# Queries as seven block products for eight, value weights in buffers of their own, two query jobs inside the attention, squares added on GpSimd

## The chip, the cores and the metric

The kernel runs on one core of one Trainium2 chip. The metric is the device time of one execution in microseconds; for the kernel before it is 1610.38 (median of three runs, 1609.49 to 1611.93). Engines go by the profile's names: PE (TensorE, with PEld for its weight loads), DVE (VectorE), ACT (ScalarE), POOL (GpSimd), SP (SyncE, here only an issuer of loads).

## The reference

One decoder layer on x of 1024 tokens x 1024 channels, in float32. Two branches (a state-space scan and an mLSTM) are merged by gates; the change begins where the merged activations are projected:

```python
x = x + merged @ w_out[l]                       # output projection
h = _rmsnorm(x, x_norm_g[l])
x = x + _cross_attn(h, _rmsnorm(mem, mem_norm_g[l]), x_wq[l], x_wkv[l], x_wo[l])
...
def _cross_attn(h, mem_n, wq, wkv, wo):         # 4 heads of 256 channels, 256 memory tokens
    q = (h @ wq).reshape(Bsz, L, X_HEADS, X_HEAD_DIM)
    k, v = jnp.split(mem_n @ wkv, 2, axis=-1)
    s = jnp.einsum('blhd,bmhd->bhlm', q, k) * (X_HEAD_DIM ** -0.5)
    o = jnp.einsum('blhm,bmhd->blhd', softmax(s), v)
    return o @ wo
```

Then a gated convolution FFN (up and down projection) and a last norm.

## The kernel before

Activations lie transposed: channels on 128 partitions, 1024 tokens along a row; a tile of 128 channels is one "n" or "k" (eight of them), the halves H0 and H1 are tokens 0 to 511 and 512 to 1023. A float32 product is made of three matmuls on rounded parts: ACT casts an operand to its high part, DVE subtracts to get the low part (`split`), and PE adds high x high, high x low and low x high (`gemm_part`). So each weight that is loaded (`load_w`: a load on SP's queue into a raw buffer WR, a cast to WH on ACT, a subtraction to WL on DVE) occupies all three engines; WR, WH and WL have two buffers each.

The stages around the change, in program order:

1. *Output projection* (`out_job`, 14 jobs). The product is made block-wise, as 2 x 2 blocks with seven products for eight (a Strassen scheme). A block splits the channels in even and odd tiles and the tokens in halves. The seven products (p = 1 to 7) take sums of the blocks of the input (`out_sums`, on DVE) and of the weight (made in DRAM by DMAs with accumulation that POOL issues long before: table Ow), and their results are added with signs when they leave PSUM. `out_x` finishes a tile half of x: DVE adds the residual, ACT and DVE make its scaled high and low part for the queries (`scaled_split`), ACT squares it, DVE adds the square to a running sum for the norm (L1064), and a DMA stores it to X1d. Products 5 and 4 are the last four jobs.
2. *Queries, keys, values.* The order is written out in the list `QKV`: q is a plain query tile (`q_tile`, 8 k-steps x 3 x 2 halves = 48 matmuls of 128x512 in an M bank of PSUM), k a key tile (24 matmuls of 128x256), v one k-step of the values (12 matmuls of 128x512 into four A banks, L1177). a0 and a1 are the first score tiles of the attention. All their weights go through WR, WH and WL.
3. *Attention.* Eight units (two token halves x four heads): scores and softmax (`att_probs`, PE, then reductions on DVE and exponentials on ACT), transposes on PE, and the product with the values (`att_values`). From the fifth unit on, the projection of the first half (`o_tile`) lies in between.
4. *FFN up and down*, again with block products for part of the columns; their weight sums (tables Uq and Dd) are made in DRAM by the same kind of DMAs.

Those DRAM sums stand in one list (`slow_sums`: 16 for the gates, 16 for Ow, 32 for Uq, 40 for Dd), and `next_sum` issues one of them at a time on POOL's queue, tied to the last matmul before it; `sums_on` switches this on in chosen stages. A build-time scheduler then sets each engine's final order within what the dependences allow, so the order on an engine is not that of the source: before, query and key tiles are interleaved on PE at places, and the last query tile stands among the first score tiles.

Buffers are pools of fixed size: S (24 of 128x1024), R (4), Z (6), VV (4), Y (18 of 128x512), and in PSUM two M and four A tiles.

## Time and profile before

| | |
|---|---|
| median of 3 runs | 1610.38 us |
| profiled execution, its own time | 1610.51 us |
| its span, first to last instruction | 1608.7 us |
| PE busy | 1581.0 us, 98%, 7935 matmuls |
| DVE busy | 1128.8 us, 70% |
| ACT busy | 752.4 us, 47% |
| POOL busy | 173.3 us, 11% |
| output projection ends | about 665 us |
| query, key and value products | about 662 to 810 us |
| attention | about 795 to 905 us |

Times in the trace count from the start of the span. "Busy" is the time in which an engine has an instruction running. A row of a timeline has start, length, engine, line, operation, output<-inputs, shapes, count, and in square brackets the idle time before it with what ended it. A row of a group has the count, the busy time, the mean of one in ns, and the idle time before it with its releasers. The chain of waits follows the work that ended last back to the start. In the names of tiles, WR<-in_w_vv_dram is a load into WR; M and A are PSUM.

### The profile page before, as it was taken

To read this page: it belongs to the slowest core of one execution; us is meant where nothing else is said; L and a number is where in the kernel's file an instruction comes from. 1 tells how busy PE (TensorE), PEld (TensorE's weight loads), DVE (VectorE), ACT (ScalarE), POOL (GpSimd) and SP (SyncE) were. 2 spreads that over 40 slices of the span, in tenths; PEclk is the share of its full clock that TensorE was granted. 3 is DMA by queue.
4 is the path that set the end of the run, shared out by engine and by line. 5 is a ranking of instruction groups with operands and counts; after the bars stand their busy time and mean duration, and the time that the engine had idled before them with its cause. 6 is when DMAs were issued, how large, how long until landed. Compare 5 with 4: busy or idle time off the path is not lost.

```text
span 1608.7 us, 21077 instructions
## 1 busy us (share of the span) xinstructions
PE 1581.0 (98%) x7935; PEld 1329.2 (83%) x7935; DVE 1128.8 (70%) x1802; ACT 752.4 (47%) x1231; POOL 173.3 (11%) x258
## 2 busy tenths in 40 slices
PE   9999999999999999999999999999999999999997
PEld 7898888888888788878888887888878888888887
DVE  7868867666565799734266469799888777867635
ACT  6446555633463437523254246444444444653413
POOL 1001111000101101000100000000111011121014
PEclk9999999999999999999999999999999999999998
DMA  6255655634987568555444458753787376876312
GB/s 196 99 147 130 154 129 127 153 99 131 294 303 183 144 156 247 182 159 157 92 140 169 128 180 254 204 150 98 208 199 192 110 183 189 295 272 210 118 40 105
DMA packets 101222, 270.55 MB, mean 168 GB/s; under 512 B 11136, under 2 KB 25152, under 8 KB 101120
## 3 DMA queue, kind: packets, MB, share of 16 engines
q1 hardware_dynamic: 66592, 160.75, 29.5%
q0 software_dynamic: 26992, 94.12, 25.8%
q10 hardware_dynamic: 7536, 14.33, 2.3%
q8 instruction: 62, 1.02, 0.3%
q14 instruction: 40, 0.33, 0.1%
HBM read 234.04 MB, written 106.43 MB: 212 GB/s over the span
## 4 chain that ended last, share of the span: by engine, by line
PE 85%; DMA 5%; DVE 4%; ACT 3%; issue 2%; POOL 0%; POOLq 0%; SPq 0%; ACTq 0%; DVEq 0%
PE M L220 29%; PE A L1408 12%; PE M L1408 10%; PE M L1555 6%; PE A L1084 5%; PE A L1555 5%; PE A L891 4%; PE A L220 3%; PE M L307 1%; DMA S<-in_w_up_dram 1%; DMA WR<-in_w_vv_dram 1%; PE A L1275 1%; PE A L1219 1%; DMA WR<-in_w_uq_dram 1%; DVE WL L185 1%
## 5 line engine op out<-in xcount | busy, mean ns | idle before, releaser
L220 PE MATMUL M<-S,WH 128*128 128x512 f32 (+1 forms) x1352 | 363.2, 381 | 3.1 <-DVE dc L802 1.4
L220 PEld LDWEIGHTS M<-S,WH 128*128 128x128 f32 x1352 | 246.4, 188 | 51.4 <-DVE Y L185 2.3
L184 ACT CAST WH<-WR 128x1024 fp32r<-128x1024 f32 (+2 forms) x115 | 109.5, 953 | 242.1 <-PE M L220 121.9
L220 PE MATMUL M<-S,WL 128*128 128x512 f32 (+1 forms) x676 | 213.3, 379 | 1.2 <-DVE WL L185 1.2
L185 DVE TENSOR_TENSOR WL<-WR,WH 128x1024 fp32r<-128x1024 f32 (+2 forms) x115 | 126.6, 1102 | 96.4 <-ACT WH L184 95.2
L220 PEld LDWEIGHTS M<-S,WL 128*128 128x128 f32 x676 | 126.9, 188 | 24.8 <-DVE WL L185 1.7
L1408 PE MATMUL M<-S,Y 128*128 128x512 f32 x468 | 111.9, 389 | 0.0
L1408 PEld LDWEIGHTS M<-S,Y 128*128 128x128 f32 x468 | 87.9, 188 | 18.2
L1431 DVE SCALAR_TENSOR_TENSOR S<-Z,cols,S 128x1023 f32<-128x1023 f32 (+1 forms) x72 | 90.8, 1280 | 7.1 <-ACT S L1429 7.0
L1408 PE MATMUL M<-S,W 128*128 128x512 f32 x324 | 78.4, 389 | 0.0
L184 ACT CAST W<-Y 128x512 fp32r<-128x512 f32 x51 | 31.6, 620 | 92.5 <-PE A L1408 74.0
L1408 PE MATMUL A<-S,W 128*128 128x512 f32 x288 | 70.9, 389 | 0.7 <-ACT W L184 0.7
L1408 PEld LDWEIGHTS M<-S,W 128*128 128x128 f32 x324 | 60.7, 188 | 12.9 <-DVE Z L1425 0.3
L1084 PE MATMUL A<-S,WH 128*128 128x512 f32 x224 | 67.7, 390 | 0.0
L891 PE MATMUL A<-S,WH 128*128 128x512 f32 x224 | 67.1, 390 | 0.0
L1408 PEld LDWEIGHTS A<-S,W 128*128 128x128 f32 x288 | 54.0, 188 | 12.2 <-ACT W L184 1.1
L211 POOL DMA_DIRECT2D Dd<-in_w_dq_dram x30 | 19.2, 642 | 388.3 <-PE M L220 134.9
L1408 PE MATMUL A<-S,Y 128*128 128x512 f32 x240 | 59.9, 389 | 0.0
L185 DVE TENSOR_TENSOR S<-S,S 128x512 fp32r<-128x512 f32 x79 | 52.2, 691 | 8.6 <-ACT S L184 8.4
L1555 PE MATMUL M<-S,W 128*128 128x512 f32 x240 | 57.8, 389 | 0.0
L1408 PE MATMUL A<-R,W 128*128 128x512 f32 x228 | 56.6, 391 | 0.3 <-ACT Z L1415 0.3
L184 ACT CAST S<-S 128x512 fp32r<-128x512 f32 x79 | 46.2, 618 | 21.2 <-PE M L1555 6.2
(509 smaller groups left out, 3401.4 us busy)
## 6 DMA issues: line engine op xcount, KB each, us to landing
Uq<-in_w_uq_dram POOLq DMA_DIRECT2D x24, 512.0 KB, 6.4
Dd<-in_w_dq_dram POOLq DMA_DIRECT2D x24, 512.0 KB, 5.1
Td<-Gq POOLq DMA_DIRECT2D x24, 512.0 KB, 8.6
WR<-in_w_in_dram SPq DMA_DIRECT2D x21, 512.0 KB, 4.1
Gq<-S SPq DMA_DIRECT2D x18, 512.0 KB, 4.6
WR<-in_w_o_dram SPq DMA_DIRECT2D x16, 512.0 KB, 3.3
...
```

The costliest lines, as they stand in the source:

```text
L184: A.copy(out=hi, in_=src)
L185: (lo_eng or V).tensor_tensor(out=lo, in0=src, in1=hi.bitcast(F32), op=ALU.subtract)
L211: d = nc.gpsimd.dma_start(out=out, in_=in_, **kw)
L220: last_mm[0] = PE.matmul(ps[:, s:e], lhsT, rhs[:, s:e], start=first and is_first, stop=last and is_last)
L307: PE.matmul(pus[j][h.start // 512], w_[:, 0, j * P : (j + 1) * P], x_[:, h], start=k == 0 and f, stop=k == KD - 1 and l)
L891: last_mm[0] = PE.matmul(ps[q], w[:, 0, c], x, start=f, stop=l, skip_group_check=True)
L1084: last_mm[0] = PE.matmul(ps[q], w[:, 0, c], x, start=f, stop=l, skip_group_check=True)
L1219: PE.matmul(ps[:, i * NM : (i + 1) * NM], lhsT[:, tok], rhs, start=f, stop=l)
L1275: last_mm[0] = PE.matmul(po, lhsT[:, ns], rhs, start=f, stop=l)
L1408: up_mm[0] = PE.matmul(ps, lhsT[:, c], rhs, start=f, stop=l, skip_group_check=True)
L1431: V.scalar_tensor_tensor(out=acc[:, d_:], in0=raw[:, : T - d_], scalar=col("fcw", 3 * ct + 2 - d_), in1=acc[:, d_:], op0=ALU.mult, op1=ALU ...
L1555: paced[0] = PE.matmul(dps[p][n], lhsT[:, c], rhs, start=f, stop=l, skip_group_check=True)
```

## The change

- *Queries as block products.* The query weights come in blocks (`w_qq`), 14 jobs (`q_job`: product p, column group g; p in the order 1, 3, 2, 6, 7, 4, 5) of 24 matmuls replace eight tiles of 48. Products 1, 3 and 2 need plain blocks of x (`out_x` makes the parts of those blocks only, 12 scaled splits for 16); 6, 7, 4 and 5 need sums, made by `q_sums` (8 ACT scalings and 16 DVE additions in all, in place in the x tiles that were stored) and split by `q_turn` (16 splits). The results are put together on leaving PSUM and split for the attention (`q_out`). The weight sums are a fourth table, Qw, with 16 more DRAM sums ahead of those for Uq.
- *Value weights.* `load_w` takes a raw buffer: value weights are loaded into Z tiles and split into VV tiles, no longer through WR, WH and WL; `qkv_weights` asks for each kind of weight one step ahead.
- *Two jobs in the attention.* Jobs 12 and 13 (product 5, for the second half of the tokens) are called in units 0 and 2.
- *Squares.* The 14 additions of squares in `out_x` are on POOL.
- *Sums.* `next_sum` is called once per query job, once in each of the first units, and behind six tiles of the second half's projection.
- The FFN, its weights and the stages before the output projection are as before.

The core of the diff:

```diff
-    "q0 k0 v0 k1 v1 q1 k2 v2 k3 v3 q2 k4 v4 k5 v5 q3 k6 v6 k7 v7 q4 q5 q6 a0 a1 q7 "
+Q_LATE = {0: 12, 2: 13}
+V_FROM = 1
+    "j0 s0 j1 k0 s1 v0 s2 j2 s3 k1 v1 t60 j3 t61 k2 t62 v2 t63 j4 x0 k3 t70 v3 t71 j5 k4 t72 v4 t73 j6 k5 t40 v5 t41 j7 t42 k6 v6 t43 j8 k7 v7 t50 j9 t51 t52 t53 j10 j11 a0 a1 "
...
-    def load_w(src, shape, alloc=None):
+    def load_w(src, shape, alloc=None, raw=None):
...
-        raw = wp.tile([P, T], F32, tag="WR", name=nm("WR"))[:, :fw]
+        raw = wp.tile([P, T], F32, tag="WR", name=nm("WR"))[:, :fw] if raw is None else raw
...
     def out_x(n, h, u, ps):
-        x = Y()
+        i, odd = n // 2, n % 2
+        x = qraw[i, odd, h] = Y() if odd or h else qe0[i // 2][:, H[i % 2]]
         V.tensor_tensor(out=x, in0=u, in1=ps, op=ALU.add)
-        hi, lo = x1g[n]
-        scaled_split(x, col("x_g", n) if n % 2 == h else nxg[:, n : n + 1], hi[:, H[h]], lo[:, H[h]])
+        if odd or not h:
+            t = (S if odd else VV)(F32R)
+            qp[1 + odd + odd * h, i] = scaled_split(x, col("x_g", n) if odd == h else nxg[:, n : n + 1], t[:, H[0]], t[:, H[1]])
...
-            V.tensor_tensor(out=sq1[h], in0=sq1[h], in1=t, op=ALU.add)
+            G.tensor_tensor(out=sq1[h], in0=sq1[h], in1=t, op=ALU.add)
...
+    def q_sums(i):
+        e0, e1, o0, o1 = (qraw[i, x, h] for x in range(2) for h in range(2))
+        n = 2 * i + 1
+        for e, g_ in ((e0, col("x_g", n - 1)), (e1, nxg[:, n - 1 : n])):
+            A.activation(out=e, in_=e, func=AF.Copy, scale=g_)
+        V.scalar_tensor_tensor(out=o1, in0=o1, scalar=nxg[:, n : n + 1], in1=e1, op0=ALU.mult, op1=ALU.add)
+        V.tensor_tensor(out=e1, in0=e0, in1=e1, op=ALU.add)
+        V.tensor_tensor(out=e0, in0=e0, in1=o1, op=ALU.add)
+        V.scalar_tensor_tensor(out=o0, in0=o0, scalar=col("x_g", n), in1=e0, op0=ALU.mult, op1=ALU.add)
...
+    def q_job(k):
+        p, g = qjobs[k]
+        wh, wl = qws.pop((p, g))
+        ps_ = psM()
+        ps = [ps_[:, H[0]], ps_[:, H[1]]]
+        for q in range(2):
+            for i in range(4):
+                c = slice(512 * q + P * i, 512 * q + P * i + P)
+                xh, xl = qp[p, i]
+                for w, x, f, l in ((wh, xh, i == 0, False), (wh, xl, False, False), (wl, xh, False, i == 3)):
+                    last_mm[0] = PE.matmul(ps[q], w[:, 0, c], x, start=f, stop=l)
+        if k in Q_SUM:
+            next_sum()
+        add, sub = ALU.add, ALU.subtract
+        if p in (1, 3):
+            t = (qu if p == 1 else qr)[g] = S()
+            A.copy(out=t, in_=ps_)
+        elif p in (6, 7):
+            V.tensor_tensor(out=qu[g], in0=qu[g], in1=ps_, op=sub if p == 6 else add)
+            if p == 6:
+                V.tensor_tensor(out=qr[g], in0=qu[g], in1=qr[g], op=sub)
+        else:
+            for q in range(2):
+                n, u = 4 * g + 2 * q, qu[g][:, H[q]]
+                if p == 2:
+                    t = Y()
+                    V.tensor_tensor(out=t, in0=u, in1=ps[q], op=add)
+                    q_out(n, 0, t)
...
+                else:
+                    r = qr[g][:, H[q]]
+                    V.scalar_tensor_tensor(out=r, in0=ps[q], scalar=-1.0, in1=r, op0=ALU.mult, op1=sub)
+                    V.tensor_tensor(out=u, in0=u, in1=ps[q], op=add)
+                    q_out(n, 1, r)
+                    q_out(n + 1, 1, u)
...
+                kvw[c, n] = load_w(a["w_vv"][n].unsqueeze(1), (1, D), VV, raw=Z())
...
-        wh, wl = load_w(a["w_vv"][k].unsqueeze(1), (1, D))
+        wh, wl = kvw.pop(("v", k))
...
         probs(u + 1, 0)
+        if u in Q_LATE:
+            q_job(Q_LATE[u])
+        elif u < 4:
+            next_sum()
         t_ = att_turn(pes.pop(u))
```

What the scheduler makes of it, at three places (names with numbers are single tiles).

PE, the end of a key tile (M_941) and the value step behind it, before; WH, WL are the shared homes:

```order
L220 MATMUL M_941_6068<-S_834_5501,WH_939_6064 128x256
L220 MATMUL M_941_6068<-S_835_5502,WH_939_6064 128x256
L220 MATMUL M_941_6068<-S_834_5501,WL_940_6065 128x256
L1177 MATMUL A_919_5941<-WH_944_6099,S_831_5482 128x512
L1177 MATMUL A_920_5942<-WH_944_6099,S_831_5482 128x512
L1177 MATMUL A_921_5943<-WH_944_6099,S_831_5482 128x512
L1177 MATMUL A_922_5944<-WH_944_6099,S_831_5482 128x512
L1177 MATMUL A_919_5941<-WL_945_6100,S_831_5482 128x512
L1177 MATMUL A_920_5942<-WL_945_6100,S_831_5482 128x512
L1177 MATMUL A_919_5941<-WH_944_6099,S_832_5483 128x512
```

PE now, around a query job (M_956, L1200); L1267 is the value step, on weights in VV:

```order
L1267 MATMUL A_911_5926<-VV_938_6060,S_831_5523 128x512
L1267 MATMUL A_912_5927<-VV_938_6060,S_831_5523 128x512
L1267 MATMUL A_911_5926<-VV_937_6059,S_832_5524 128x512
L1267 MATMUL A_912_5927<-VV_937_6059,S_832_5524 128x512
L1200 MATMUL M_956_6183<-S_866_5731,WH_945_6123 128x512 x2
L1267 MATMUL A_909_5924<-VV_950_6158,S_831_5523 128x512
L1267 MATMUL A_910_5925<-VV_950_6158,S_831_5523 128x512
L1200 MATMUL M_956_6183<-S_866_5731,WL_946_6124 128x512
L1200 MATMUL M_956_6183<-S_870_5744,WH_945_6123 128x512 x2
L1200 MATMUL M_956_6183<-S_870_5744,WL_946_6124 128x512
```

The value matmuls no longer read WH and WL, and two of the next step stand between the query job's first matmuls and those that need its low weights WL_946.

DVE at the end of the output projection, from the first eviction of product 5 (A_881), before; L1064 adds squares, WL_892 is a weight of the last output jobs:

```order
L1056 TENSOR_TENSOR Y_883_5746<-S_782_5224,A_881_5720 128x512
L1056 TENSOR_TENSOR Y_884_5752<-S_818_5427,A_881_5720 128x512
L275 SCALAR_TENSOR_TENSOR S_870_5702<-Y_883_5746,cols_75,S_869_5701 128x512
L1056 TENSOR_TENSOR Y_886_5760<-S_782_5224,A_882_5721 128x512
L275 SCALAR_TENSOR_TENSOR VV_773_5186<-Y_884_5752,nxg_4846,VV_772_5185 128x512
L1064 TENSOR_TENSOR Z_720_4845<-Z_720_4845,Y_885_5756 128x512
L1056 TENSOR_TENSOR Y_888_5768<-S_818_5427,A_882_5721 128x512
L185 TENSOR_TENSOR WL_892_5779<-WR_890_5776,WH_891_5778 128x1024
L1056 TENSOR_TENSOR Y_896_5813<-S_789_5270,A_894_5787 128x512
L275 SCALAR_TENSOR_TENSOR S_872_5704<-Y_886_5760,cols_75,S_871_5703 128x512
L1064 TENSOR_TENSOR Z_720_4845<-Z_720_4845,Y_887_5764 128x512
L275 SCALAR_TENSOR_TENSOR VV_775_5188<-Y_888_5768,nxg_4846,VV_774_5187 128x512
```

DVE now, from the same eviction (A_863); L1171 to L1173 are sums of query inputs:

```order
L1060 TENSOR_TENSOR Y_865_5729<-S_776_5219,A_863_5703 128x512
L1060 TENSOR_TENSOR Y_867_5736<-S_808_5418,A_863_5703 128x512
L252 TENSOR_SCALAR ms_836_5560<-M_837_5561 128x2
L278 SCALAR_TENSOR_TENSOR S_866_5731<-Y_865_5729,cols_75,S_866_5731 128x512
L1060 TENSOR_TENSOR Y_869_5742<-S_776_5219,A_864_5704 128x512
L1060 TENSOR_TENSOR Y_872_5751<-S_808_5418,A_864_5704 128x512
L188 TENSOR_TENSOR WL_876_5760<-WR_874_5757,WH_875_5759 128x1024
L278 SCALAR_TENSOR_TENSOR S_870_5744<-Y_869_5742,cols_75,S_870_5744 128x512
L1060 TENSOR_TENSOR Y_880_5794<-S_783_5265,A_878_5768 128x512
L1171 SCALAR_TENSOR_TENSOR Y_865_5729<-Y_865_5729,nxg_4847,Y_867_5736 128x512
L1060 TENSOR_TENSOR Y_883_5803<-S_818_5467,A_878_5768 128x512
L1172 TENSOR_TENSOR Y_867_5736<-R_721_4849,Y_867_5736 128x512
```

POOL now, at the same time:

```order
L253 TENSOR_TENSOR rm_4851<-ms_836_5560,mhalf_99 128x2
L1069 TENSOR_TENSOR Z_720_4846<-Z_720_4846,Y_868_5738 128x512
L1069 TENSOR_TENSOR Z_720_4846<-Z_720_4846,Y_871_5747 128x512
L1069 TENSOR_TENSOR Z_720_4846<-Z_720_4846,Y_873_5753 128x512
L1069 TENSOR_TENSOR Z_720_4846<-Z_720_4846,Y_882_5799 128x512
L1069 TENSOR_TENSOR Z_720_4846<-Z_720_4846,Y_884_5805 128x512
L1069 TENSOR_TENSOR Z_720_4846<-Z_720_4846,Y_887_5814 128x512
L1069 TENSOR_TENSOR Z_720_4846<-Z_720_4846,Y_889_5820 128x512
```

The square additions have left DVE for POOL, where seven follow each other behind the norm of the memory; in their place DVE has the input sums.

PE at the first score tiles (L1219, the last query tile M_1051 behind them), before:

```order
L1219 MATMUL A_1045_6864<-Z_722_4852,S_927_6002 128x256
L1219 MATMUL A_1045_6864<-R_721_4851,S_927_6002 128x256
L1219 MATMUL A_1045_6864<-R_721_4851,S_950_6172 128x256
L1219 MATMUL A_1045_6864<-Z_722_4852,S_950_6172 128x256
L1219 MATMUL A_1045_6864<-R_721_4851,S_950_6172 128x256
L220 MATMUL M_1051_6891<-VV_772_5185,WH_1049_6887 128x512 x2
L220 MATMUL M_1051_6891<-VV_773_5186,WH_1049_6887 128x512 x2
L220 MATMUL M_1051_6891<-VV_772_5185,WL_1050_6888 128x512 x2
```

PE now: score tiles (L1305), then job 12 (M_1103):

```order
L1305 MATMUL A_1100_6969<-R_933_6045,S_976_6312 128x256
L1305 MATMUL A_1100_6969<-R_933_6045,S_1065_6853 128x256
L1305 MATMUL A_1100_6969<-Z_934_6046,S_1065_6853 128x256
L1305 MATMUL A_1100_6969<-R_933_6045,S_1065_6853 128x256
L1200 MATMUL M_1103_6990<-S_1050_6769,WH_1095_6959 128x512 x2
L1200 MATMUL M_1103_6990<-S_1050_6769,WL_1096_6960 128x512
L1200 MATMUL M_1103_6990<-S_1055_6805,WH_1095_6959 128x512 x2
L1200 MATMUL M_1103_6990<-S_1055_6805,WL_1096_6960 128x512
```

Where one query tile stood there are now the two jobs of product 5, M_1103 and, behind it, M_1134.

More of the change, by code (lines that the diff above doesn't have):

```diff
@@ L220, in gemm_part, with ntile @@
                 last_mm[0] = PE.matmul(ps[:, s:e], lhsT, rhs[:, s:e], start=first and is_first, stop=last and is_last)
-    def ntile(src, xs, nk=KD, width=T, w=None, order=None):
+    def ntile(src, xs, nk=KD, width=T, w=None):
         wh, wl = w or load_w(src, (nk, P))
         ps = psM()
-        for i, k in enumerate(order or range(nk)):
-            gemm_part(ps, (wh[:, k, :], wl[:, k, :]), xs[k][0], xs[k][1], width, i == 0, i == nk - 1)
-            if i % 4 == 3:
-                next_sum(i // 4)
+        for k in range(nk):
+            gemm_part(ps, (wh[:, k, :], wl[:, k, :]), xs[k][0], xs[k][1], width, k == 0, k == nk - 1)
+            if k % 4 == 3 and width == T:
+                next_sum(k // 4)
         return ps
@@ new lines, in hybrid_layer, with qkv_weights @@
+    Kt, kv_k = [None, None], {}
+    kvw, asked = {}, set()
+    def qkv_weights(i, kinds, ahead):
+        for step in QKV[i:]:
+            c, n = step[0], int(step[1:])
+            if c not in kinds:
+                continue
+            if not ahead:
+                break
+            ahead -= 1
+            if step in asked:
+                continue
+            asked.add(step)
+            if c == "j":
+                q_weights(n)
+            elif c == "k":
+                kvw[c, n] = load_w(a["w_k"][n], (KD, P))
+            else:
+                kvw[c, n] = load_w(a["w_vv"][n].unsqueeze(1), (1, D), VV, raw=Z())
@@ L1163, in k_tile @@
     def k_tile(n):
-        ps = ntile(a["w_k"][n], mhv, width=NM)
+        ps = ntile(None, mhv, width=NM, w=kvw.pop(("k", n)))
+        Kt[n // 4] = Kt[n // 4] or (R(F32R), Z(F32R))
+        kv_k[n] = [t[:, (n % 4) * NM : (n % 4) * NM + NM] for t in Kt[n // 4]]
         kf = Y()[:, :NM]
@@ L1187, in hybrid_layer @@
     sums_on[0] = 0
-    x1g += [(VV(F32R)[:, :T], VV(F32R)[:, :T]) if n in (0, 2) else None for n in range(KD)]
     for k, (p, g) in enumerate(ojobs):
@@ L1193, in hybrid_layer @@
             out_turn(OUT_TURNS[k])
-        if k in (2, 10):
-            for n in range(k == 10, KD, 2):
-                x1g[n] = x1g[n] or (S(F32R), S(F32R))
         if k == MEM_AT:
@@ L1232, in hybrid_layer @@
     pv = [psA() for _ in range(4)]
-    for step in QKV:
-        n = int(step[1])
+    sums_on[0] = 1
+    qkv_weights(0, "j", 1)
+    for i_, step in enumerate(QKV):
+        n = int(step[1:])
+        if step[0] in "jkv":
+            qkv_weights(i_ + 1, "jk", 1)
+            if i_ > V_FROM:
+                qkv_weights(i_ + 1, "v", 1)
         if step[0] == "k":
             k_tile(n)
-        elif step[0] == "q":
-            q_tile(n)
+        elif step[0] == "x":
+            x1_norm()
+        elif step[0] == "s":
+            q_sums(n)
+        elif step[0] == "t":
+            q_turn(n // 10, n % 10)
+        elif step[0] == "j":
+            k = n
+            q_job(k)
         elif step[0] == "a":
-            if not n:
-                x1_norm()
             pes.setdefault(0, []).append(att_probs(2 * n, 0))
@@ L1581, in weights @@
             down_w(k - len(jobs))
+    for k in Q_LATE.values():
+        q_weights(k)
+    sums_on[0] = 0
     units = [(half, h) for half in range(2) for h in range(4)]
```

55 lines of the change are left out of this document (34 added, 21 removed).

## Prediction

> **What bounds the kernel now.** I read the page first, then the busy time by stage, then the chain of waits, then single stretches in order of time. The page gives the bound at once:
>
> ```profile
> PE 1581.0 (98%) x7935; PEld 1329.2 (83%) x7935; DVE 1128.8 (70%) x1802; ACT 752.4 (47%) x1231; POOL 173.3 (11%) x258
> ```
>
> PE is busy for 98% of the span, so the time is the number of matmuls times their pace, plus the few places where PE waits. The busy time by stage (span of the stretch, then PE, PEld, DVE, ACT and POOL busy with their counts, granted clock, DMA share, GB/s) shows where the change works: output projection to 662, query, key and value products to 810, attention to 905, then the joint of the last two, and ten-microsecond pieces of the end of the output projection.
>
> ```profile
> 582.00:662.00 80.00, 79.75 (x356) 65.81 (x355) 71.11 (x109) 55.19 (x96) 7.94 (x11) 1.00 0.68 211
> 662.00:810.00 148.00, 143.87 (x731) 120.33 (x730) 58.45 (x84) 45.30 (x68) 11.95 (x17) 1.00 0.52 139
> 810.00:905.00 95.00, 93.64 (x518) 80.36 (x517) 62.60 (x113) 48.14 (x108) 2.61 (x4) 1.00 0.45 150
> 800.00:840.00 40.00, 38.64 (x236) 33.56 (x235) 25.86 (x54) 21.84 (x58) 3.31 (x5) 1.00 0.39 97
> 650.00:660.00 10.00, 10.00 (x46) 8.28 (x45) 10.00 (x16) 9.14 (x15) 0.00 (x0) 1.00 0.58 192
> 660.00:670.00 10.00, 10.00 (x46) 8.29 (x45) 10.00 (x15) 6.85 (x11) 0.00 (x0) 1.00 0.58 203
> ```
>
> PE hardly rests anywhere, at a granted clock of 1.00. DVE has room in the query stage (58.45 of 148 us) and none at all from 650 to 670 us, where the output projection ends. What a matmul costs stands in the chain of waits, where PE runs without a wait (start, length, line, count):
>
> ```profile
> 647.87 14.54 PE A L1084 x64
> ...
> 761.36 32.65 PE M L220 x144
> ```
>
> The second row is three whole query tiles: 32.65/144 = 0.227 us for a 128x512 matmul; the first, in the output projection, gives the same 14.54/64 = 0.227.
>
> **Part 1: fewer matmuls.** A query tile has 8 k-steps x 3 products x 2 halves = 48 matmuls, eight tiles 384. The seven block products have 2 column groups x 2 x 4 x 3 = 24 matmuls in each of 14 jobs, 336. So 48 go: 48 x 0.227 = **-10.9 us**. The new program's PE has 48 instructions fewer (7498 for 7546 in order), and all those removed were at the full 512 width, on the engine that sets the end; nothing hides them.
>
> **Part 2: value weights.** In order of time, PE's key tile and the value step behind it:
>
> ```profile
> 679.18 1.19 PE L1177 MATMUL A<-WH,S 128*128 128x512 f32 x4 [0.25 <-ACT WH L184]
> ...
> 683.24 0.40 PE L220 MATMUL M<-S,WH 128*128 128x256 f32 x2
> ...
> 685.64 0.28 PE L220 MATMUL M<-S,WL 128*128 128x256 f32 x1
> 688.06 1.20 PE L1177 MATMUL A<-WH,S 128*128 128x512 f32 x4 [2.14 <-ACT WH L184]
> ```
>
> ```profile
> PE A L1177 <- ACT WH L184: 3.2, 3, 2.1
> ```
>
> ```profile
> DMA to landing us min/median/max: 3.5/4.6/6.5
> ```
>
> PE stood 2.14 us for the cast of a value weight, whose load had taken 3.5 to 6.5 us to land (last row, of the value-weight loads), since loads of queries, keys and values share two raw and two split homes. The rows from 679.18 to the three query tiles at 761.36 (82.2 us) hold eight value steps (96 matmuls at 0.227 = 21.8), three query tiles (144, 32.7) and seven key tiles (168 at 0.12, from 20 matmuls between 683.24 and 685.64: 20.2): 74.7 us. So 7.6 us are lost there, the visible waits and the slow first matmuls behind them (1.20 us for four). With a home of its own a value weight is loaded and split some steps ahead, and the new order of PE even slips single value matmuls into a query job while its low part is being made. But 14 query jobs instead of 8 tiles make more joints of two short pieces, each with a fresh weight. Bounds: 0 to 7.6 us back; I take **-4.5**, most of the value waits and not the joints.
>
> **Part 3: what DVE and ACT get.** Durations:
>
> ```profile
> L185 DVE TENSOR_TENSOR WL<-WR,WH 128x1024 fp32r<-128x1024 f32 x91 | 111.1, 1222 | 93.9 <-ACT WH L184 92.7 <-issue 0.6 <-PE A L307 0.5
> L184 ACT CAST WH<-WR 128x1024 fp32r<-128x1024 f32 x91 | 95.5, 1051 | 225.2 <-PE M L220 112.6 <-issue 28.6 <-PE A L220 15.8
> ...
> L185 DVE TENSOR_TENSOR S<-Y,S 128x512 fp32r<-128x512 f32 x40 | 26.2, 689 | 3.6 <-ACT S L184 3.5
> ...
> L1760 POOL TENSOR_TENSOR Z<-Z,Y 128x512 f32<-128x512 f32 x7 | 9.1, 1296 | 61.7 <-ACT Y L1756 61.2
> ```
>
> DVE: 6 more weights split (x 1.22 = 7.3), 16 sums of inputs and 16 splits of them (32 x 0.69 = 22.1), 6 evictions of 1024 (7.3) and 16 of 512 (11.0), 4 scaled splits fewer (-2.8): +44.9 us, and 14 squares fewer (-9.7). ACT: 6 casts, 4 copies of 1024, 20 more of 512, about +23. From 662 to 905 DVE is busy 121 of 243 us; 35 more leave it at two thirds. Step by step it also fits: behind a job of products 2 or 4 DVE has two evictions and one weight to do (2 x 0.6 + 1.14 at the pace below, 2.3 us) while PE does a key tile (24 x 0.12 = 2.9 us). So I put this part at 0, covered by key tiles; without that cover a job would lose up to 2.3 us.
>
> **Part 4: squares on GpSimd.** Fourteen additions of 1.296 us move to POOL, which has room. What they may cost shows at the end of the program, where POOL adds squares already (first row POOL, the others DVE; start, length):
>
> ```profile
> 1570.73 4.05 POOL L1760 TENSOR_TENSOR Z<-Z,Y 128x512 f32<-128x512 f32 x3 [3.46 <-ACT Y L1756]
> ```
>
> ```profile
> 1571.70 0.41 DVE L1751 TENSOR_TENSOR VV<-VV,A 128x256 f32<-128x256 f32 x1
> 1572.89 0.42 DVE L1751 TENSOR_TENSOR VV<-VV,M 128x256 f32<-128x256 f32 x1 [0.78 <-PE M L220]
> 1573.80 1.27 DVE L1760 TENSOR_TENSOR Z<-Z,Y 128x256 f32<-128x256 f32 x1 [0.48 <-ACT Z L1753]
> 1574.99 0.41 DVE L1751 TENSOR_TENSOR VV<-VV,M 128x256 f32<-128x256 f32 x1
> 1575.32 0.41 DVE L1760 TENSOR_TENSOR Z<-Z,Y 128x256 f32<-128x256 f32 x1
> ```
>
> While POOL added (until 1574.78), the DVE additions that read one operand from PSUM (VV,A and VV,M) took their usual 0.41; the one with both operands in SBUF took 1.27 and ended just after POOL did; the same addition later took 0.41. So DVE loses about 0.9 us to a POOL addition whenever its next operation reads SBUF twice. Eleven of the fourteen fall in the last four output jobs, where DVE is full, and the order puts the new sums and the weight splits among them, which all read SBUF twice. DVE's pace there:
>
> ```profile
> 646.10 1.29 DVE L1056 TENSOR_TENSOR Y<-S,A 128x512 f32<-128x512 f32 x2 [1.13 <-PE A L1084]
> ...
> 667.14 0.69 DVE L1056 TENSOR_TENSOR Y<-S,A 128x512 f32<-128x512 f32 x1
> 667.73 1.23 DVE L185 TENSOR_TENSOR WL<-WR,WH 128x1024 fp32r<-128x1024 f32 x1
> 668.87 0.76 DVE L275 SCALAR_TENSOR_TENSOR S<-Y,nxg,S 128x512 fp32r<-128x512 f32 x1
> 669.53 0.69 DVE L1064 TENSOR_TENSOR Z<-Z,Y 128x512 f32<-128x512 f32 x1
> ```
>
> From start to start: 0.60 for an addition of 512, 1.14 for a weight, 0.66 for a scaled one. From the eviction of product 5 (646.10) to the low part of the first query job's weights the new order has 9 evictions and 5 sums at 0.60, 7 scaled operations at 0.66, 3 weights at 1.14: 16.4 us, with about 1 us of waiting for PE, ready at 663.5. PE needs it when the output projection ends, about 665.5: 2 us of slack. Some eight of the eleven POOL additions lie before that point, three more before the next job's weights. Below: 0, if they meet evictions only or POOL lags. Above: 11 x 1.296 - 2 = 12.3. I take 11 x 0.9 = 9.9 less the 2 of slack and about 2.5 that the key and value steps behind the first two jobs absorb: **+5.5 us**. In the measured stretches up to 646 PE lost nothing to a full DVE, so the 9.7 us that DVE is spared buy nothing.
>
> [...]
>
> **Part 5: two jobs in the attention.** The last jobs (product 5) are only needed by the second half of the tokens and fill PE where softmax waits. Before, the eighth query tile did that: 40 us at the joint hold 1.36 us of idle PE. But the tile cost DVE one weight and two splits (2.6 us), the two jobs cost two weights, eight evictions, eight splits (13.5 us), in order ahead of reductions and transposes that PE waits for. In 810 to 905 DVE has 32 us free, so at most a few single waits: 0 to 4, I take **+1.5**.
>
> **Part 6: loads.** Six more weight loads of 512 KB and 16 more DRAM sums. The sums push the last 16 of the table Uq behind them, into the query jobs and attention:
>
> ```profile
> L1377 SPq DMA_DIRECT2D Y<-Uq x32: 319/320/656, 973.6 to 1062.7; - x32
> L211 POOL DMA_DIRECT2D Uq<-in_w_uq_dram x24: 520/542/844, 356.9 to 582.4; - x24
> ```
>
> They are read from 973.6 on and would be issued until about 840: over 100 us of slack, and a DMA share of 0.52 there. Cost 0; if a raw weight came late instead, each would be a wait like the 2.14 above.
>
> **The sum** goes against the profiled execution: it took 1610.51 us, its span 1608.7; the median of three runs is 1610.38, so the two agree. 1610.5 - 10.9 - 4.5 + 5.5 + 1.5 = **1602.1**; I say 1602.
>
> **Rivals.** *Full gain* (25%): POOL's additions meet evictions, or DVE runs ahead. For it: 9 of the 24 DVE operations in that stretch read PSUM, POOL waits for ACT's squares. Against: DVE is 100% busy there. Without the 5.5 and with 1 in the attention: 1610.5 - 10.9 - 4.5 = 1595 to 1596. *Full lock* (17%): each of the eleven holds DVE for 1.296 us and PE follows, +12.3, and half the value gain goes (2.2): 1610.5 - 10.9 - 2.3 + 12.3 = 1609.6, with the attention's wait 1610; no difference. [...] Against: additions that fall beside evictions. *Joints* (10%): the slower side. Query jobs of 5.4 us and key tiles of 2.9 us go through two homes for split weights, and a weight can only be split once its home is free: 1.05 cast and 1.22 subtraction, 2.3 us, then evictions before it on DVE. If each of the 14 jobs loses 1.7 us at its start, that is 23.8 against 15.4 gained: 1610.5 - 15.4 + 23.8 = 1619. It decides from 15.4/14 = 1.1 us a job. For it: key joints of 2.9 us; against: the count in part 3 fits. That the change does not do what it says is no rival: the matmul count is fixed.
>
> **How the numbers follow.** Forecast 1602 (48%, own range 1598 to 1607). What a measurement of this kernel can tell from no change is about 0.2%, 3.2 us. Faster by more: 47 of the forecast, 25, and 3 of full lock: 0.75. Within: 1 and 13: 0.14. Slower: 1 and 10: 0.11. The range 1594 to 1611 leaves out the joints and the tail of the full gain.
>
> **What would show it.** PE's matmuls 48 fewer, about 0.227 each. No PE wait for value weights over 1 us. POOL additions between 648 and 675, and among them DVE operations with two SBUF inputs at 1.3 to 2 us instead of 0.69, then PE waiting for the low part of the last output weight or the first two query weights, some 5 us in all. If DVE's rows there keep their length, part 4 is wrong; if PE waits at each query job through the stage, the joints decide.

## The result, and the profile after

The change makes the kernel slower: 1620.55 us (median of 6 runs, 1617.93 to 1623.66) against 1612.10 us (6 runs, 1609.49 to 1613.55); the ratio is 1.0056 with a 95% interval of 1.0041 to 1.0071, some 9 us. The forecast was 1602 us and faster. The profiled execution of the changed kernel took 1621.01 us, its span is 1619.2; that of before was 1608.7.

The page's first line, and the stretches shown of before (same columns):

```profile
PE 1575.9 (97%) x7887; PEld 1323.6 (82%) x7887; DVE 1168.5 (72%) x1844; ACT 772.6 (48%) x1261; POOL 206.8 (13%) x288
```

```profile
582.00:662.00 80.00, 77.91 (x342) 62.65 (x341) 65.74 (x97) 51.74 (x91) 17.22 (x18) 1.00 0.68 205
662.00:810.00 148.00, 142.41 (x755) 122.06 (x754) 107.47 (x149) 72.94 (x114) 24.02 (x23) 0.99 0.56 159
810.00:905.00 95.00, 89.89 (x468) 75.98 (x467) 61.14 (x106) 45.38 (x96) 5.98 (x9) 0.98 0.61 182
650.00:660.00 10.00, 10.00 (x47) 8.31 (x48) 8.40 (x12) 6.29 (x11) 5.42 (x4) 1.00 0.72 221
660.00:670.00 10.00, 7.37 (x25) 5.34 (x24) 9.43 (x10) 7.73 (x13) 6.21 (x4) 0.83 0.44 143
```

PE has its 48 matmuls fewer (7887 records for 7935), but now it rests in stretches where it was full: 2.6 us from 660 to 670, with a granted clock of 0.83 beside it, and 5.1 us for 1.4 in the attention. To see all of it I took, over every matmul record, the time from its start to the next one's start, less the median of that time for its shape, and summed the excess by stretch. It holds PE's waits and a slower pace alike; "lost" means this number from here on.

| us lost by PE in | 604–700 | 700–790 | 790–905 | 905–985 | 985–1180 | 1180–1390 |
|---|---|---|---|---|---|---|
| before | 4.2 | 3.6 | 2.8 | 1.3 | 1.3 | 1.2 |
| after | 10.8 | 0.2 | 8.8 | 4.8 | 1.2 | 9.0 |

The query stage proper lost nothing any more. What was gained was given back in three other places: the end of the output projection, the attention, and the up projection, where no line of the code was changed.

**The end of the output projection.** Timeline rows of ACT, then of PE (the longest of three waits for later output weights up to 632 us):

```profile
610.96 0.72 ACT L1170 ACTIVATE R<-R,cols 128x512 f32<-128x512 f32 x1 [2.17 <-DMA X1d<-R]
...
613.86 1.03 ACT L187 CAST WH<-WR 128x1024 fp32r<-128x1024 f32 x1
```

```profile
630.19 0.50 PE L1092 MATMUL A<-S,WL 128*128 128x512 f32 x1 [1.13 <-DVE WL L188]
```

L1170 is the scaling in `q_sums`. It writes into the tile of x that it reads, so it has to wait until the store of x has read that tile; behind it on ACT stands the cast of the next output weight. Later the same, with DVE behind ACT (ACT, then DVE, then PE):

```profile
659.82 0.72 ACT L1170 ACTIVATE Y<-Y,nxg 128x512 f32<-128x512 f32 x1 [2.69 <-DMA X1d<-Y]
```

```profile
660.57 0.75 DVE L1171 SCALAR_TENSOR_TENSOR Y<-Y,nxg,Y 128x512 f32<-128x512 f32 x1 [1.54 <-ACT Y L1170]
...
663.62 1.76 DVE L1172 TENSOR_TENSOR Y<-R,Y 128x512 f32<-128x512 f32 x1
665.31 1.21 DVE L188 TENSOR_TENSOR WL<-WR,WH 128x1024 fp32r<-128x1024 f32 x1
```

```profile
666.58 0.79 PE L1092 MATMUL A<-S,WL 128*128 128x512 f32 x1 [1.89 <-DVE WL L188]
667.17 1.05 PE L1092 MATMUL A<-S,WH 128*128 128x512 f32 x2
```

Both things show in DVE's rows: the wait for the scaling (1.54), and a sum that takes 1.76 us for 0.68 beside an addition of GpSimd. PE then waits 1.89 us for the low part, and the next matmuls are slower (1.05 for two, 0.62 usually), at a granted clock of 0.50 from 667 to 669.

**The attention.** Issues of the DRAM sums and of the first loads of the attention's output weights (POOL, SP), the cast that waits for it, PE:

```profile
819.12 0.81 POOL L214 DMA_DIRECT2D Uq<-Uq  x1 [3.79 <-issue]
822.09 0.54 POOL L214 DMA_DIRECT2D Dd<-in_w_dq_dram  x1 [2.17 <-PE A L1372]
823.45 0.53 POOL L214 DMA_DIRECT2D Dd<-in_w_dq_dram  x1 [0.81 <-PE A L1305]
```

```profile
823.66 0.83 SPq L196 DMA_DIRECT2D WR<-in_w_o_dram  x2
```

```profile
832.31 1.04 ACT L187 CAST WH<-WR 128x1024 fp32r<-128x1024 f32 x1 [6.25 <-DMA WR<-in_w_o_dram]
```

```profile
833.41 1.01 PE L223 MATMUL M<-S,WH 128*128 128x512 f32 x2 [3.70 <-ACT WH L187]
```

The load was issued at 823.66, its cast starts at 832.31: 8.6 us, with three sums issued in the five us before it. In the kernel before, the same load was issued at 829.83 and its cast started at 834.85, 5.0 us, beside one sum per six us:

```profile
829.83 0.82 SPq L193 DMA_DIRECT2D WR<-in_w_o_dram  x2
```

```profile
834.85 1.05 ACT L184 CAST WH<-WR 128x1024 fp32r<-128x1024 f32 x1 [2.54 <-DMA WR<-in_w_o_dram]
```

**The up projection.** The sums for the down projection (table Dd) by tile, before and after, then a weight load of the up projection and who waits for it:

```profile
L211 POOL DMA_DIRECT2D Dd<-in_w_dq_dram x30: 520/555/856, 671.0 to 1132.6; - x30
```

```profile
L214 POOL DMA_DIRECT2D Dd<-in_w_dq_dram x30: 528/548/1118, 822.1 to 1249.8; - x30
```

```profile
1181.31 0.33 SPq L1479 DMA_DIRECT2D S<-in_w_up_dram  x1
```

```profile
1190.97 0.69 DVE L1483 TENSOR_TENSOR Y<-S 128x512 f32<-128x512 f32 x1 [9.05 <-DMA S<-in_w_up_dram]
```

```profile
1198.00 4.61 PE L1505 MATMUL A<-R,W 128*128 128x512 f32 x12 [4.37 <-ACT Z L1512]
```

The sums are one queue. Sixteen more of them ahead (Qw) pushed the last of these from 1133 to 1250 us; of all 40 for Dd ten are issued after 1145 us, one before the change. There the FFN's own transfers (Gq, Td) are dense: before the change the DMA share is 0.85 from 1145 to 1180 us, against 0.52 from 662 to 810. The load takes 9.6 us, only one more than the same load before (8.6 us). But it is also issued 5.5 us later, as soon as a store to Gq has landed, and that store took 7.3 us for 2.7, beside a sum for Dd issued at 1173.62 (SP, before, then now):

```profile
1173.09 0.38 SPq L1443 DMA_DIRECT2D Gq<-S  x1
1175.76 0.33 SPq L1382 DMA_DIRECT2D S<-in_w_up_dram  x1
```

```profile
1173.96 0.38 SPq L1540 DMA_DIRECT2D Gq<-S  x1
```

DVE's sum of weights comes late by both, ACT's copy behind it too, and PE waits 4.4 us.

### The profile page after: what moved, and what is told of

The parts are those of the page before. It is cut to its first block, busy times and chain, and to the rows that moved or that the text cites. A ratio compares the mean times of both kernels' runs of the same rounds, so it can differ in the third digit from the quotient of the medians.

```text
span 1619.2 us, 21148 instructions
## 1 busy us (share of the span) xinstructions
PE 1575.9 (97%) x7887; PEld 1323.6 (82%) x7887; DVE 1168.5 (72%) x1844; ACT 772.6 (48%) x1261; POOL 206.8 (13%) x288
## 4 chain that ended last, share of the span: by engine, by line
PE 79%; DVE 8%; DMA 7%; ACT 4%; issue 2%; POOL 0%; ACTq 0%; POOLq 0%; SPq 0%; DVEq 0%
PE M L223 25%; PE A L1505 11%; PE M L1505 9%; PE M L1652 6%; PE A L1652 5%; PE A L895 4%; PE M L1200 4%; PE A L223 2%; DMA S<-in_w_up_dram 2%; PE A L1267 1%; PE M L310 1%; DMA WR<-in_w_uq_dram 1%; PE A L1372 1%; DVE WL L188 1%; ACT S L187 1%
## 5 line engine op out<-in xcount | busy, mean ns | idle before, releaser
L223 PE MATMUL M<-S,WH 128*128 128x512 f32 (+1 forms) x1160 | 312.2, 380 | 5.8 <-ACT WH L187 4.0
L223 PEld LDWEIGHTS M<-S,WH 128*128 128x128 f32 x1160 | 211.6, 189 | 45.8 <-ACT WH L187 4.6
L223 PE MATMUL M<-S,WL 128*128 128x512 f32 (+1 forms) x580 | 184.3, 378 | 1.3 <-DVE WL L188 1.3
L223 PEld LDWEIGHTS M<-S,WL 128*128 128x128 f32 x580 | 109.1, 189 | 21.6 <-DVE WL L188 2.2
L1200 PE MATMUL M<-S,WH 128*128 128x512 f32 x192 | 59.3, 390 | 0.0
L1505 PEld LDWEIGHTS A<-R,W 128*128 128x128 f32 x228 | 43.6, 192 | 17.6 <-ACT Z L1512 8.4
```

The lines of the kernel that those rows point to most:

```text
L223: last_mm[0] = PE.matmul(ps[:, s:e], lhsT, rhs[:, s:e], start=first and is_first, stop=last and is_last)
L1200: last_mm[0] = PE.matmul(ps[q], w[:, 0, c], x, start=f, stop=l)
L1505: up_mm[0] = PE.matmul(ps, lhsT[:, c], rhs, start=f, stop=l, skip_group_check=True)
```

## The experiments

Thirteen kernels; each is compared with the kernel before on the same chip. Most executions of a kernel lie within 5 us of its median, a few are 10 us off, and differences between two of these kernels under 2 us are not told apart. The last three columns are the us lost by PE in these stretches. They come from one profiled execution each: before 604 us, where the code is nearly the same in all, these lose 13.7 to 17.7 us, so that 1 or 2 us say little here too. The profiled executions of sums_early and before_sq_pool were the fastest of their twelve (1607.4 and 1606.7), those of fresh_nolate and fresh_v_shared the slowest of their six (1608.9 and 1623.5). The kernels from fresh_placed on in the table all have the edit of fresh.

| kernel | median us | ratio to before | 604–700 | 790–985 | 1180–1390 |
|---|---|---|---|---|---|
| before | 1612 | | 4.2 | 4.1 | 1.2 |
| after | 1620.6 | 1.0056 (1.0041–1.0071) | 10.8 | 13.6 | 9.0 |
| sq_dve | 1618.9 | 1.0045 (1.0029–1.0061) | 11.6 | 11.3 | 8.0 |
| store_other | 1623.3 | 1.0070 (1.0043–1.0097) | 11.7 | 10.3 | 12.3 |
| store_other_sq | 1610.6 | 0.9997 (0.9982–1.0012) | 5.5 | 10.3 | 6.2 |
| sums_held | 1611.2 | 0.9993 (0.9979–1.0008) | 1.4 | 11.1 | 8.9 |
| fresh | 1607.9 | 0.9978 (0.9966–0.9989) | 0.0 | 11.3 | 7.8 |
| before_sq_pool | 1610.4 | 0.9989 (0.9979–0.9999) | 3.9 | 3.5 | −0.2 |
| sums_early | 1611.1 | 1.0003 (0.9988–1.0018) | 10.5 | 8.6 | −0.3 |
| all3 | 1605.9 | 0.9970 (0.9959–0.9981) | 5.3 | 7.0 | 6.0 |
| fresh_placed | 1601.4 | 0.9934 (0.9919–0.9949) | 0.0 | 5.5 | 3.8 |
| fresh_placed2 | 1594.5 | 0.9895 (0.9872–0.9919) | 0.0 | 5.5 | 1.9 |
| placed2_sq_dve | 1596.5 | 0.9899 (0.9875–0.9922) | 0.2 | 5.5 | 2.3 |
| fresh_v_shared | 1623.4 | 1.0052 (1.0033–1.0070) | 1.7 | 8.8 | 13.3 |
| fresh_nolate | 1606.1 | 0.9961 (0.9946–0.9975) | 0.0 | 16.6 | 3.8 |

### What is lost at the end of the output projection

Three things meet there. The *store wait* is that of the in-place scaling for the store of the same tile. The *hold* is the lengthening of DVE's operations beside GpSimd's additions (1.76 us for 0.68 above). The *place* is that scalings and sums stand among the work of the output projection at all.

**sq_dve** undoes part 4.

```diff
-            G.tensor_tensor(out=sq1[h], in0=sq1[h], in1=t, op=ALU.add)
+            V.tensor_tensor(out=sq1[h], in0=sq1[h], in1=t, op=ALU.add)
```

> The changed kernel with the 14 additions of squares back on DVE; nothing else. Theory lock (POOL's additions hold DVE's two-SBUF operations: eleven of them show 0.4 to 1.1 us over their usual length between 650 and 687 us, about 8 us in all, and PE then waits for low parts of weights): PE's losses of 4.8 us (632 to 674) and 2.8 us (674 to 700) shrink by about half, 1620.5 goes to 1615 to 1618. Rival store wait (ACT is held 2.2 and 2.7 us because the in-place scaling of the query sums waits for the store of the same tile, and the weight casts stand behind it): the losses stay, DVE has 9.7 us more to do, 1620 to 1622.

The loss stayed (11.6 for 10.8), 1618.9 us, between the ranges of the two theories. DVE's operations have their usual length again (0.68 us for such a sum, 1.21 to 1.23 for a weight), but DVE stands at the scaling (ACT, then DVE of this kernel):

```profile
662.88 0.72 ACT L1170 ACTIVATE Y<-Y,nxg 128x512 f32<-128x512 f32 x1 [3.33 <-DMA X1d<-Y]
```

```profile
663.64 0.75 DVE L1171 SCALAR_TENSOR_TENSOR Y<-Y,nxg,Y 128x512 f32<-128x512 f32 x1 [2.69 <-ACT Y L1170]
```

That spoke for the store wait.

**fresh** gives the scaled values a tile of their own.

```diff
-        x = qraw[i, odd, h] = Y() if odd or h else qe0[i // 2][:, H[i % 2]]
+        x = qraw[i, odd, h] = Y()
...
-        for e, g_ in ((e0, col("x_g", n - 1)), (e1, nxg[:, n - 1 : n])):
-            A.activation(out=e, in_=e, func=AF.Copy, scale=g_)
+        f0, f1 = qraw[i, 0, 0], qraw[i, 0, 1] = qe0[i // 2][:, H[i % 2]], Y()
+        for f, e, g_ in ((f0, e0, col("x_g", n - 1)), (f1, e1, nxg[:, n - 1 : n])):
+            A.activation(out=f, in_=e, func=AF.Copy, scale=g_)
+        e0, e1 = f0, f1
```

> The changed kernel with the scaling for the query sums written to a tile of its own, not in place, so that ACT has not to wait for the store of the unscaled tile. Theory store wait: ACT's idle times of 2.2 us (609 us) and 2.7 us (657 us) before a scaling go, PE's loss of 3.2 us between 604 and 632 goes and 1 to 2 us of the next 4.8: 1620.5 goes to 1615 to 1617.5. Rival lock: the loss at 604 to 632 comes from POOL's addition that held DVE 1.1 us at 608.4, nothing changes by more than 1 us: 1619.5 to 1621.5.

The whole loss went, 1607.9 us, where 1615 to 1617.5 was expected. The first scaling no longer waits (ACT), but the sums had moved as well (DVE): the first of them now stands behind the whole output projection.

```profile
608.51 0.71 ACT L1171 ACTIVATE R<-Y,cols 128x512 f32<-128x512 f32 x1
```

```profile
673.37 0.74 DVE L1173 SCALAR_TENSOR_TENSOR Y<-Y,nxg,Y 128x512 f32<-128x512 f32 x1
```

So this kernel did not tell the store wait from the place of the sums. GpSimd's additions are all still there and cost PE nothing (0.0 us lost from 604 to 700).

**store_other** takes the store wait away (for 14 of the 16 stores) and leaves scalings and sums where they are. It stores the square in place of x, so its output is another one; the work and the traffic are the same.

```diff
         if fresh_sq[h]:
+            t = x
             A.activation(out=sq1[h], in_=x, func=AF.Square)
...
-        A.dma_start(out=X1d[n][:, H[h]], in_=x)
+        A.dma_start(out=X1d[n][:, H[h]], in_=t)
```

> The changed kernel, except that 14 of the 16 stores of x read the tile with its square and not x itself, so that the in-place scalings wait for no store; the stored values, and so the output, are other ones, the work and the traffic are the same. The sums for the queries stay where the changed kernel has them, among DVE's evictions at the end of the output projection. Theory store wait alone: ACT's idle times before the scalings go, the losses of 3.2 us (604 to 632) and of 7.6 us (632 to 700) both go nearly to 0, 1620.5 goes to 1610 to 1612. Theory two causes (the store wait makes the first loss, the eleven sums among a full DVE the second; the tile of its own had removed both, since the sums then stood behind the output projection): the first goes, 4 to 7 us of the second stay, 1615 to 1618.

The theory of the store wait alone fell: 11.7 us lost. Its 1623.3 us lie above both ranges, in part by the up projection (12.3 for 9.0), which this edit does not touch. GpSimd's hold took the place of the store (DVE, ACT, and DVE again, 50 us later):

```profile
606.83 1.81 DVE L278 SCALAR_TENSOR_TENSOR VV<-R,cols,VV 128x512 fp32r<-128x512 f32 x1
```

```profile
609.25 0.72 ACT L1171 ACTIVATE R<-R,cols 128x512 f32<-128x512 f32 x1 [2.05 <-DVE R L1060]
```

```profile
659.62 1.78 DVE L1174 TENSOR_TENSOR R<-R,Y 128x512 f32<-128x512 f32 x1
```

The split of x on DVE took 1.81 us for 0.75. By the trace the in-place scaling then stood 2.05 us for the eviction (L1060) that follows this split on DVE and ends at 609.24. In the changed kernel the same eviction ended at 610.83, and the scaling that had waited for the store started at 610.96: the two waits lay side by side.

**sums_held** changes the place alone: in place, squares on GpSimd, but scalings and sums held back behind the first query jobs. **store_other_sq** keeps the place and takes both waits away (the edits of store_other and sq_dve together; its output is another one too). The edit of sums_held:

```diff
-            A.activation(out=e, in_=e, func=AF.Copy, scale=g_)
+            d = A.activation(out=e, in_=e, func=AF.Copy, scale=g_)
+            tc.add_manual_dep(d.ins, last_mm[0].ins.name, DependencyInfo(DependencyClass.Sync, DependencyReason.DATA), reason="late")
```

> The changed kernel, scaling in place and squares on GpSimd as there; only the eight scalings, and so the sixteen sums behind them, are held back until the first query job has ended, so that neither stands in the output projection. Theory place (the loss of 10.8 us from 604 to 700 comes from scalings and sums standing among the work that PE waits for, on ACT where they wait for readers and stores of x, on DVE where there is no time for them): losses from 604 to 700 under 1 us, 1620.5 goes to 1607 to 1610, as with a tile of its own. Rival in-place: with in-place scaling the waits only move behind the first query job, where casts and low parts of the next weights wait instead, 3 us or more stay there: 1612 to 1618.

> The changed kernel with both waits away, while scalings and sums keep their place among the evictions: stores read the tile of the square (other values are stored, so the output is another), and squares are added on DVE, not on GpSimd. If store wait and hold by GpSimd each cover for the other (removing one alone gave nothing): losses from 604 to 700 fall from 10.8 to under 4 us, 1609 to 1613. If DVE simply has no time there for the eleven sums: 6 us or more stay between 632 and 700, 1614 to 1620.

Held back, the loss falls from 10.8 to 1.4 us, in one wait at 635, and the time to 1611.2 us (1607 to 1610 expected). PE's busy time from 604 to 674, of the changed kernel and of this one:

```profile
604.00:674.00 70.00, 65.52 (x279) 51.98 (x278) 58.60 (x81) 49.71 (x87) 23.38 (x20) 0.98 0.68 207
```

```profile
604.00:674.00 70.00, 68.93 (x307) 56.70 (x307) 61.65 (x81) 49.55 (x87) 28.81 (x23) 1.00 0.71 226
```

So the place costs, and writing in place costs next to nothing elsewhere. With both waits away at the old place, 632 to 700 loses 2.7 us; with the store wait alone away it was 8.3, with the hold alone away 8.5, with neither away 7.6. Each covers for the other. (From 604 to 700 store_other_sq still loses 5.5 us, not the under 4 expected. 2.8 of them lie before 632, behind a wait of 1.42 us for one of the two stores that still read x; that this wait makes all of them is not shown.) Twelve of the sixteen sums came to where eleven squares had been, about 0.6 us each, so DVE had as much to do as before, when it was busy 100% of 650 to 670: its work just fits, and a hold or a wait on top of it goes to PE.

**before_sq_pool** is the kernel before with part 4 alone (the edit of sq_dve the other way).

> The kernel before with one edit of the change, the 14 additions of squares on GpSimd. Theory lock (part 4 of the prediction): DVE is busy 100% of 650 to 672, POOL's additions hold its two-SBUF operations, PE waits at the end of the output projection: 1611.5 goes to 1614 to 1618. Theory store wait (the changed kernel lost its time there by the in-place scaling alone): DVE's lengthened operations show in the trace, but DVE is also spared 9.7 us, PE loses nothing from 582 to 674: 1610 to 1612.

The hold shows as the prediction read it (2.17 us for a weight that took 1.23), and PE does wait for it (DVE, then PE):

```profile
656.86 2.17 DVE L185 TENSOR_TENSOR WL<-WR,WH 128x1024 fp32r<-128x1024 f32 x1
```

```profile
659.09 0.50 PE L1084 MATMUL A<-S,WL 128*128 128x512 f32 x1 [0.63 <-DVE WL L185]
```

From 632 to 674 PE lost 2.5 us where it had lost none, but from 674 to 700 it lost 1.5 for 4.2: the value weight that PE had stood 2.14 us for in the kernel before came in time for the later start, but for 0.42 us. In all part 4 alone is worth at most 0.2% (0.9989, 0.9979 to 0.9999), on the faster side. Neither theory had it whole.

### What is lost from the attention on

**sums_early** issues one more sum behind each key tile and each value step.

```diff
         ps = ntile(None, mhv, width=NM, w=kvw.pop(("k", n)))
+        next_sum()
...
-                    PE.matmul(pv[2 * m + j], lhsT, rhs[:, 0, 512 * j : 512 * j + 512], start=k == 0 and f, stop=k == KD - 1 and l)
+                    last_mm[0] = PE.matmul(pv[2 * m + j], lhsT, rhs[:, 0, 512 * j : 512 * j + 512], start=k == 0 and f, stop=k == KD - 1 and l)
+        next_sum()
```

> The changed kernel with one more weight sum issued behind each key tile and each value step (16 more in the query stage), so that the sums for the down projection are issued 16 places earlier; none then falls after about 1145 us, where ten do now (one before the change). Theory late sums (these transfers delay the weight loads of the up projection, PE waits 4.8 us at 1193 and 2.9 us at 1251 and then runs at a lower clock for some us): the losses after 1145 us go, 1620.5 goes to 1608 to 1613. Rival: the up projection's own traffic makes the waits, or the sums do the same harm in the query stage (30 sums in 148 us): 1617 to 1624.

1611.1 us, and the loss after 1180 is gone (−0.3 in its fastest execution). The attention is another matter: the queue stands 16 places further on there too, yet 790 to 905 still lose 7.7 us for 8.8, and the first output weight takes 7.2 us to land. There it is not the push that costs, but the calls in the first units, which issue sums beside that load. PE's busy time from 1180 to 1390, changed kernel and this one:

```profile
1180.00:1390.00 210.00, 203.13 (x888) 167.09 (x887) 168.00 (x225) 91.85 (x136) 29.38 (x44) 0.99 0.69 186
```

```profile
1180.00:1390.00 210.00, 210.00 (x928) 173.96 (x927) 173.16 (x230) 99.70 (x145) 28.23 (x44) 1.00 0.66 186
```

**all3** has the edits of sq_dve, fresh and sums_early.

> The changed kernel with all three edits: squares on DVE, sums 16 places earlier, scaling not in place. If the three causes are separate and add: 1620.5 - 3.5 - 9.5 - 4 = 1603 to 1604, and faster than the kernel before by 0.5%. If lock and store wait are one loss told twice (either repair gives nearly all of it): 1607. If the sums do harm in the query stage: 1612 or more.

The gains did not add: fresh and sums_early alone are 12.7 and 9.5 us faster than the changed kernel, which together would give 1598; measured are 1605.9. Sixteen more sums in the query stage made a value weight late (PE waits 3.3 us up to 694), and one wait of the up projection came back at 1196 us, though no sum for Dd is issued there any more. The hidden blocks' own sums (Td) are the only ones there, so PE's wait there (2.10 us) came without Dd; why this kernel had it and the fastest execution of sums_early had not stays open.

**fresh_placed** and **fresh_placed2** are fresh with the sums put where the profile shows room, and with none in the first five attention units; the second also makes the doubled pace reach the jobs it was meant for.

```diff
         ps = ntile(None, mhv, width=NM, w=kvw.pop(("k", n)))
+        if n > 2:
+            next_sum()
...
     for u in range(len(units)):
+        sums_on[0] = int(u > 4)
...
         last_mm[0] = up_mm[0]
+        sums_on[0] = 2 if 30 <= k < 72 else 4
         next_sum(k)
```

The first piece stands in the value step too; the last is that of fresh_placed2.

> The changed kernel with the scaling not in place, and the sums put where the transfers have room: ten more in the query stage (behind key tiles and value steps 3 to 7), none in the first five attention units, twice as many in the stretch of the up projection from about 1065 to 1145 us. All sums are then issued by about 1150 us. Theory late sums: the load of the first output weight in the attention lands in 5 us for 8.6, PE's losses from 790 to 830 fall from 9.4 to 3 to 5 us, those from 1180 to 1300 from 7.0 to 1 or 2 us; 1607.9 goes to 1595 to 1599. Rival: these waits come from other traffic (the up projection's own stores and sums of hidden blocks, reads of x), and the sums in the query stage cost as much there: 1604 to 1609.

> As the kernel with the sums placed anew, but with the doubled pace of the sums reaching the jobs it was meant for (in that kernel it sat in a loop that ends before them), so that no sum for the down projection is issued once those of the hidden blocks begin (about 1135 us). Theory late sums: PE's waits of 3.2 us each at 1173 and 1230 us go, 1601.4 goes to 1593 to 1596. Rival: the hidden blocks' own sums make these waits: 1599 to 1602.

The first gave 1601.4, not the 1595 to 1599 expected: the attention's part held (3.1 us lost from 790 to 905 for 9.4, and the first output weight landed in 3.3 us), but the up projection still waited twice. The second gave **1594.5 us**, 0.9895 of the kernel before (0.9872 to 0.9919). Its sums by tile, and the stretches of attention and up projection:

```profile
L214 POOL DMA_DIRECT2D Dd<-in_w_dq_dram x30: 531/579/892, 762.7 to 1103.8; - x30
```

```profile
790.00:905.00 115.00, 113.24 (x605) 96.61 (x604) 74.89 (x132) 53.72 (x115) 4.96 (x6) 1.00 0.44 143
...
1180.00:1390.00 210.00, 208.33 (x919) 171.94 (x918) 175.02 (x236) 100.88 (x152) 28.40 (x46) 1.00 0.65 190
```

**placed2_sq_dve** is that kernel with the squares on DVE.

> The kernel of the run fresh_placed2 with the 14 additions of squares back on DVE. If GpSimd's additions cost PE nothing where DVE has room (part 4 of the change is worth 0): within 1.5 us of that kernel. If they hold DVE to PE's cost: 2 to 5 us faster. If they spare DVE where it is full: 2 to 5 us slower.

1596.5 for 1594.5, with intervals that overlap: with the rest mended no effect of part 4 can be told from scatter.

### The two other parts

**fresh_v_shared** is fresh with the value weights back in the shared homes, and asked for in one row with the others.

```diff
-                kvw[c, n] = load_w(a["w_vv"][n].unsqueeze(1), (1, D), VV, raw=Z())
+                kvw[c, n] = load_w(a["w_vv"][n].unsqueeze(1), (1, D))
...
-            qkv_weights(i_ + 1, "jk", 1)
-            if i_ > V_FROM:
-                qkv_weights(i_ + 1, "v", 1)
+            qkv_weights(i_ + 1, "jkv", 1)
```

> The changed kernel with the scaling not in place and with the value weights again in the shared raw and split buffers, as before the change. Theory (part 2): value steps and query jobs wait for each other's weights, PE loses 5 to 10 us between 674 and 790 where it loses 0.15 now: 1607.9 goes to 1613 to 1618. Rival: with query jobs of 5.4 us between them the casts come in time: 1607 to 1610.

It lost 10.5 us from 604 to 790 where fresh lost 0.15, and took 1623.4 us. PE from 674 to 790, of fresh and of this kernel:

```profile
674.00:790.00 116.00, 116.00 (x628) 100.74 (x627) 81.72 (x116) 56.29 (x85) 10.29 (x13) 1.00 0.58 171
```

```profile
674.00:790.00 116.00, 109.23 (x569) 92.41 (x568) 74.87 (x100) 50.48 (x69) 8.56 (x11) 0.99 0.59 169
```

The theory of part 2 held, for homes and asking ahead together; this run does not part them. The time is above the 1613 to 1618 expected: in this profile, the slowest of its six executions, another 5 us lie after 1180 (13.3 lost for 7.8).

**fresh_nolate** is fresh with the last two query jobs moved ahead of the attention.

```diff
-Q_LATE = {0: 12, 2: 13}
+Q_LATE = {}
...
-    "... t52 t53 j10 j11 a0 a1 "
+    "... t52 t53 j10 j11 j12 j13 a0 a1 "
```

> The changed kernel with the scaling not in place and with query jobs 12 and 13 in front of the first score tiles, not inside the attention. If the two late jobs cost PE little (part 5, 0 to 4 us) and fill waits of the softmax: 1607.9 goes to 1607 to 1612, with the attention's losses as large or larger by the 10.9 us of work that no longer fills it. If they are what delays the attention (the 9.4 us lost from 790 to 830): 1600 to 1604.

1606.1 us for 1607.9, not told apart. In the profile the attention loses 15.1 us for 9.4, and the up projection 3.8 for 7.8. So in the attention the late jobs do cover some 5 us of waits, and are not what delays it.

## Why the prediction was wrong, by its own steps

- **The bound** was read rightly: everything went by what PE waits for.
- **Part 1** (−10.9) held. In the chain of the changed kernel two query jobs are one piece of 48 matmuls, again at 0.227 us:

```profile
772.01 10.88 PE M L1200 x48
```

- **Part 2** (−4.5, bounds 0 to 7.6): mechanism right, size too small. Where nothing else stands in the way (fresh) the losses of 4.2 and 3.6 us are gone but for 0.2: −7.6. The joints that I held back for cost nothing. (82.2 less 74.7 is 7.5, not 7.6; it changes nothing.)
- **Part 3** (0) is the first step that failed. Its cover, key tiles, was argued for the query stage, and there nothing was lost (0.2 us from 700 to 790), although the count left out the two splits behind the evictions of a job. But the eight scalings and twelve of the sums do not stand there; on DVE they stand ahead of the last eviction of the output projection, in an order that was printed ahead of the prediction. It gave the in-place scaling no wait, neither for the store nor for DVE's split of the same tile, and did not ask what is queued behind it on ACT: the casts of output weights. Measured, with part 4: 10.8 us from 604 to 700.
- **Part 4** (+5.5): the hold is there as read; in the changed kernel, from 650 to 687 us, DVE's operations beside GpSimd's additions took 0.4 to 1.1 us over their usual length. The count of DVE's work (2 us of slack) fits up to 674, where store_other_sq, with both waits away, loses 0.4 us; behind it, up to 700, another 2.3 are lost, which the count did not have. Beside the sums, with the store wait away, the hold is worth 8.3 - 2.7 = 5.6 us in the two profiles, the size forecast. But as the change stands the store wait covers it (undoing part 4 gives 1.7 us, within scatter), and alone, before the change or after the repair, it moves the time by no more than scatter.
- **Part 5** (+1.5, 0 to 4): nothing speaks against it. Moving the jobs out gives −1.8 us, within scatter, and with the sums away (fresh_placed) the attention with both jobs in it loses 3.1 us, for 2.8 before the change.
- **Part 6** (0) is the second step that failed, and the larger. It asked when the pushed sums of Uq are read (973.6) and found slack, and it asked neither what is pushed behind them nor what else travels where sums are issued. The longer queue pushed what stood behind it: the last sums of Dd went from 1133 to 1250 us and landed on the dense transfers of the FFN (1180 to 1390: +7.8; gone in sums_early). And the new calls in the first units issue sums beside the load of the first output weights (790 to 905: +6.0; gone in fresh_placed, but not in sums_early). That is 13.8 us. Another 3.5 us were lost at the joint to the up projection (905 to 985); no run shows that the sums make them, since store_other and sums_held, with the same calls, lose 0.9 us there, less than the 1.3 of before. That cause stays open.
- **The sum** with measured terms: 1608.7 − 10.9 − 7.6 + 10.8 + 13.8 + 3.5 = 1618.3, against a span of 1619.2.
- **The rivals.** "Joints" had the number (1619) by luck and not the mechanism: it put the loss into the query jobs, which lost nothing. "Full lock" overrated the hold: no run shows that each addition holds DVE for its whole 1.296 us; in the changed kernel the eleven made some 8 us, 1.1 us at most for one of DVE's operations. A late transfer far behind the change was no rival at all, and it should have been one.

Both faults can be mended without giving up the change: with the scaling out of place and the sums placed by room, it is worth 17 us, where the forecast was 8.
